# Eight heads instead of four on the partitions for Q and the output of a linear attention, with more stores held back

## The chip, the cores and the metric

The kernel runs on one core of a Trainium2 chip. The metric is the device time of one execution in microseconds (us), which is lower when better. Times are medians of several runs. A profile shows one execution, and its span is 1.8 us shorter than that execution's time (129.1 of 130.87 us before). The engines are PE (matrix multiply), DVE (VectorE), ACT (ScalarE), POOL (GpSimd) and SP (SyncE). In the profile of the kernel before, GpSimd's transfers stand in a queue of the kind software (q0, 20.98 MB) and SP's and ACT's in two of the kind hardware (q1, 10.49 MB, and q10, 0.52 MB). Their packets took 81.7%, 21.7% and 1.1% of the time of the same 16 DMA engines; that is over 100% together, since packets overlap.

## The reference

```python
# Q, K, V: (8, 12, 512, 64) float32
Q_feat = np.maximum(0, Q)
K_feat = np.maximum(0, K)
KV = np.einsum('bhkd,bhkv->bhdv', K_feat, V)
K_sum = np.sum(K_feat, axis=2)
numerator = np.einsum('bhqd,bhdv->bhqv', Q_feat, KV)
denominator = np.einsum('bhqd,bhd->bhq', Q_feat, K_sum)
out = numerator / (denominator[:, :, :, None] + 1e-10)
```

There are 96 heads. The work per byte is small: 37.7 MB are read and 12.6 MB written.

## The kernel before

Four heads make a group, and there are 24 groups. A group's Q, K, V and output lie on 128 partitions, 32 partitions a head, so each partition holds one contiguous row of 4 KB in HBM. The loads cast to bf16 and are issued by GpSimd. PE computes K-transposed times V for the group (line 120, 32 matmuls), transposes Q (line 135, 8), and multiplies (line 150, 32). A column of ones beside V gives the denominator.

```python
def load_kv(g):                                   # ... K, V: [P, 16 rows, 64] bf16
    nc.gpsimd.dma_start(out=k_sb[g].rearrange("p r d -> p (r d)"), in_=Kr[g])
    ...
def mm_kv(g):
    for r in range(R):                            # R = 16
        for t in range(2):                        # two halves of 64 partitions
            ts_ = slice(64 * t, 64 * t + 64)
            nc.tensor.matmul(ps_kv[g][:, t, 0:D1],
                kf[g][ts_, r, :, :].rearrange("p s d -> p (s d)"),
                vo[g % NB][ts_, r, :],
                start=(r == 0), stop=(r == R - 1), skip_group_check=True)
def mm_out(g):
    for j in range(2):
        ...
            for h in range(NHG):                  # 4 heads, one strip of 32 columns each
                hs = slice(32 * h, 32 * h + 32)
                nc.tensor.matmul(po[hs, v // 2, ...], qt[g][:, u, hs],
                    kvd[g % NB][:, h // 2, h % 2, :, :],
                    start=True, stop=True, skip_group_check=True)
def store(g, o_sb):
    if NG - 2 - HELD <= g < NG - 2:               # HELD = 5
        nc.gpsimd.dma_start(out=Or[g], ...)       # behind all loads, in GpSimd's program
    elif g == NG - 1:
        ...                                       # two halves, nc.sync
    else:
        nc.sync.dma_start(out=Or[g], ...)
```

Stores of five late groups are "held": GpSimd issues them after the last load, so that they do not compete with loads that the computation needs: in the trace a group takes 3.75 us where loads run alone and 5.11 us where stores run beside them.

## Time and profile before

| | before |
|---|---|
| time, median (3 runs) | 131.06 us |
| span in the profile | 129.1 us |
| PE busy, instructions (matmuls; as many weight loads) | 76.5 us, 1728 |
| granted PE clock (mean share of full speed) | 0.573 |
| HBM read, written | 37.75 MB, 12.58 MB |

The first lines of the page of the kernel before: busy time by engine, then the granted clock and the DMA engines' busy share in 40 slices (9 is 90% or more), and further down the chain that ended last.

```profile
PE 76.5 (59%) x1728; PEld 57.0 (44%) x1728; DVE 79.8 (62%) x230; ACT 51.1 (40%) x121; POOL 45.1 (35%) x81
...
PEclk9999955555555555555555555555555555555785
DMA  4999999999999999999999999999999999999972
...
DMA 86%; issue 3%; PE 3%; POOL 2%; DVE 2%; ACT 2%; ACTq 0%; POOLq 0%
```

No compute engine is over 62% busy, the DMA engines are full from the second slice to the 38th, and the chain is DMA. The kernel is bound by its transfers.

Windows of the kernel before (start and end, length, busy time of each engine with its count of instructions, then granted clock, DMA share, GB/s as counted at the landing side, where a load counts as bf16, half of what it reads from HBM: the packets of the whole run hold 32.23 MB, where 50.3 MB were read and written in HBM; a share above 1, such as 1.12 from 108 to 110 us, says that the times of packets overlap).

```profile
120.00:122.00 2.00, 1.67 (x40) 1.29 (x32) 1.35 (x6) 1.05 (x5) 0.24 (x1) 0.67 1.00 399
122.00:124.00 2.00, 0.64 (x32) 0.46 (x32) 1.31 (x4) 0.79 (x1) 0.00 (x0) 1.00 0.70 285
124.00:126.00 2.00, 0.00 (x0) 0.00 (x0) 1.40 (x4) 0.00 (x0) 0.00 (x0) 0.68 0.82 329
126.00:128.00 2.00, 0.00 (x0) 0.00 (x0) 0.00 (x0) 0.00 (x0) 0.00 (x0) 0.50 0.41 157
```

In the last 6 us the DMA engines have a hole: the last groups' stores come one by one as they are computed.

### The profile page before, as it was taken

The numbers are of one execution on the slowest core, as the hardware profiler recorded it, in microseconds if no ns is written. First come the engines' busy times: TensorE is split into PE (matmuls) and PEld (weight loads), VectorE is DVE, ScalarE is ACT, GpSimd is POOL, SyncE is SP. The second block draws the span as 40 slices with busy tenths as digits, with TensorE's granted clock in tenths as the row PEclk, the third lists the DMA queues.
The fourth block names the chain that finished last, engine by engine and source line by source line (L and its number), as shares of the span: only waits on it lengthen the run. The fifth ranks groups of instructions, "written<-read, shape, count | busy, mean of one in ns | idle before, by whom it ended". The sixth has DMA issues, their size and how long they took to land.

```text
span 129.1 us, 4091 instructions
## 1 busy us (share of the span) xinstructions
PE 76.5 (59%) x1728; PEld 57.0 (44%) x1728; DVE 79.8 (62%) x230; ACT 51.1 (40%) x121; POOL 45.1 (35%) x81
## 2 busy tenths in 40 slices
PE   0068476547576585485675755855756458887610
PEld 0057354425444363364454544633644336665410
DVE  1283775737757558467476584584673849889660
ACT  3027535433345334433543453344335253652700
POOL 6945343133333315224333243152331335311100
PEclk9999955555555555555555555555555555555785
DMA  4999999999999999999999999999999999999972
GB/s 118 305 209 209 211 171 274 277 219 285 229 269 272 226 285 250 245 286 239 258 282 225 275 262 234 285 249 248 285 230 267 273 227 206 212 216 368 388 307 111
DMA packets 13986, 32.23 MB, mean 250 GB/s; under 512 B 1553, under 2 KB 1553, under 8 KB 13969
## 3 DMA queue, kind: packets, MB, share of 16 engines
q0 software_dynamic: 10800, 20.98, 81.7%
q1 hardware_dynamic: 3024, 10.49, 21.7%
q10 hardware_dynamic: 144, 0.52, 1.1%
q8 instruction: 13, 0.21, 0.6%
q14 instruction: 5, 0.03, 0.1%
HBM read 37.75 MB, written 12.58 MB: 390 GB/s over the span
## 4 chain that ended last, share of the span: by engine, by line
DMA 86%; issue 3%; PE 3%; POOL 2%; DVE 2%; ACT 2%; ACTq 0%; POOLq 0%
DMA q_sb<-in_Q_dram 38%; DMA k_sb<-in_K_dram 27%; DMA v_sb<-in_V_dram 21%; ACT qt L139 2%; PE ps_qt L135 1%; PE ps_out L150 1%; DVE o_sb L164 1%; POOL q_sb L80 0%; POOL v_sb L76 0%; POOL k_sb L74 0%; DVE rec L163 0%; POOL ident masks.py:199 0%; DVE den L161 0%; POOL ident masks.py:197 0%; ACTq L139 0%
## 5 line engine op out<-in xcount | busy, mean ns | idle before, releaser
L120 PE MATMUL ps_kv<-vo,kf 64*128 64x65 bf16 x768 | 25.1, 239 | 36.3 <-DVE vo L112 34.4
L120 PEld LDWEIGHTS <-kf 64*128 64x128 bf16 x768 | 21.4, 126 | 42.0 <-DVE vo L112 34.3
L129 ACT CAST kvd<-ps_kv 64x130 bf16<-64x130 f32 x96 | 25.3, 264 | 36.1 <-PE ps_kv L120 34.2
L139 ACT ACTIVATE qt<-ps_qt 128x1024 bf16<-128x1024 bf16 x24 | 24.6, 1023 | 33.8 <-PE ps_qt L135 33.8
L110 DVE TENSOR_SCALAR kf<-k_sb,mask 128x1024 bf16<-128x1024 bf16 x46 | 20.3, 483 | 27.2 <-DMA k_sb<-in_K_dram 27.2
L150 PE MATMUL ps_out<-kvd,qt 128*32 128x130 bf16 x768 | 28.8, 303 | 10.0 <-DVE o_sb L164 6.9
L164 DVE TENSOR_TENSOR o_sb<-ps_out,rec 128x512 f32<-128x512 f32 x48 | 33.2, 692 | 1.7
L80 POOL DMA_DIRECT2D q_sb<-in_Q_dram x24 | 17.2, 715 | 36.0 <-DMA k_sb<-in_K_dram 34.7
L150 PEld LDWEIGHTS <-qt 128*32 128x32 bf16 x768 | 17.4, 127 | 18.8 <-DVE o_sb L164 12.5
L135 PE MATMUL ps_qt<-ident,q_sb 128*128 128x128 bf16 x192 | 24.3, 306 | 0.7 <-DMA q_sb<-in_Q_dram 0.7
L135 PEld LDWEIGHTS <-q_sb 128*128 128x128 bf16 x192 | 18.1, 139 | 5.5 <-issue 4.4
L76 POOL DMA_DIRECT2D v_sb<-in_V_dram x23 | 12.3, 533 | 19.3 <-DMA q_sb<-in_Q_dram 15.0
L74 POOL DMA_DIRECT2D k_sb<-in_K_dram x23 | 12.4, 541 | 11.8 <-DMA v_sb<-in_V_dram 8.9
L112 DVE COPY vo<-v_sb 128x1024 bf16<-128x1024 bf16 x23 | 9.9, 431 | 8.5 <-DMA v_sb<-in_V_dram 8.5
L163 DVE RECIPROCAL rec<-den 128x8 f32<-128x8 f32 x48 | 9.7, 203 | 1.7
L161 DVE TENSOR_SCALAR den<-ps_out 128x8 f32<-128x8 f32 x48 | 7.5, 157 | 1.7 <-PE ps_out L150 1.7
L174 POOL DMA_DIRECT2D out_dram<-o_sb x5 | 2.7, 549 | 7.8 <-DVE o_sb L164 6.2
L110 DVE TENSOR_SCALAR kf<-k_first,mask 128x1024 bf16<-128x1024 f32 x2 | 1.4, 751 | 3.8 <-DMA k_first<-in_K_dram 3.8
L129 ACT ACT_TABLE_LOAD x1 | 1.3, 1283 | 1.8 <-DVE kvd L103 1.8
L101 DVE MEMSET mask<- 32x1 f32 x8 | 0.3, 59 | 0.9 <-PEq L213 0.8
L103 DVE MEMSET kvd<- 128x260 f32 x3 | 0.8, 275 | 0.0
L112 DVE CAST vo<-v_first 128x1024 bf16<-128x1024 f32 x1 | 0.7, 692 | 0.0
(7 smaller groups left out, 1.1 us busy)
## 6 DMA issues: line engine op xcount, KB each, us to landing
out_dram<-o_sb SPq DMA_DIRECT2D x18, 512.0 KB, 6.9
q_sb<-in_Q_dram POOLq DMA_DIRECT2D x24, 256.0 KB, 12.4
k_sb<-in_K_dram POOLq DMA_DIRECT2D x23, 256.0 KB, 13.7
v_sb<-in_V_dram POOLq DMA_DIRECT2D x23, 256.0 KB, 13.7
out_dram<-o_sb POOLq DMA_DIRECT2D x5, 512.0 KB, 9.6
v_first<-in_V_dram ACTq DMA_DIRECT2D x1, 512.0 KB, 4.8
k_first<-in_K_dram SPq DMA_DIRECT2D x1, 512.0 KB, 4.7
out_dram<-o_sb SPq DMA_DIRECT2D x2, 256.0 KB, 2.4
```

Source lines behind the costliest of these rows:

```text
L74: nc.gpsimd.dma_start(out=k_sb[g].rearrange("p r d -> p (r d)"), in_=Kr[g])
L76: nc.gpsimd.dma_start(out=v_sb[g].rearrange("p r d -> p (r d)"), in_=Vr[g])
L80: nc.gpsimd.dma_start(out=q_sb[g].rearrange("p u f -> p (u f)"), in_=Qr[g])
L110: nc.vector.tensor_scalar(kf[g][:, :, s, :], k_sb[g], scalar1=0.0, scalar2=mask[:, s:s + 1], op0=Alu.max, op1=Alu.mult)
L112: nc.vector.tensor_copy(vo[g % NB][:, :, 0:D], v_sb[g])
L120: nc.tensor.matmul(ps_kv[g][:, t, 0:D1], kf[g][ts_, r, :, :].rearrange("p s d -> p (s d)"), vo[g % NB][ts_, r, :], start=(r == 0), stop=(r ...
L129: nc.scalar.copy(kvd[g % NB][64 * c:64 * c + 64, :, s, c, :], ps_kv[g][64 * s:64 * s + 64, :, 0:D1])
L135: nc.tensor.transpose(ps_qt[g][:, u, :], q_sb[g][:, u, :], ident)
L139: nc.scalar.activation(qt[g].rearrange("p u q -> p (u q)"), ps_qt[g].rearrange("p u q -> p (u q)"), Act.Relu)
L150: nc.tensor.matmul(po[hs, v // 2, (v % 2) * 2 * D1:(v % 2) * 2 * D1 + 2 * D1], qt[g][:, u, hs], kvd[g % NB][:, h // 2, h % 2, :, :], start ...
L163: nc.vector.reciprocal(rec, den)
L164: nc.vector.tensor_tensor(o_sb[:, 8 * j:8 * j + 8].rearrange("p (b r) d -> p b r d", b=2), pv[:, :, :, 0:D], rec.unsqueeze(3).to_broadcast ...
```

## The change

The intent: longer rows for half of the bytes (Q and output in "octets" of eight heads, 16 partitions a head, 8 KB rows), and more stores held behind the loads to fill the hole at the end. A strip of 32 PE columns now holds two heads. So the transposed Q is written twice, each time with the other head's columns zero, and two matmuls accumulate: 1536 output matmuls instead of 768. The diff, cut to its core:

```diff
-    NHG = 4
-    R = S * NHG // P
-    U = R // 2
+    R = S * 4 // P                      # K, V: 16
+    RQ = S * 8 // P                     # Q, out: 32
+    U = RQ // 2
+    NO = NG // 2                        # 12 octets
+    F32 = 2
-    qin = pool("qin", NG)
-    kin = pool("kin", 20)
-    outp = pool("outp", 10)
+    qin = pool("qin", 7)
+    kin = pool("kin", 12)
+    outp = pool("outp", HELD + 2)       # 8 KB tiles, HELD = 5 octets
...
+    for g in range(F32):                # K, V of groups 0 and 1 in fp32, by SP and ACT
+        nc.sync.dma_start(out=k_sb[g]..., in_=Kr[g])
+        nc.scalar.dma_start(out=v_sb[g]..., in_=Vr[g])
...
+    def evac_qt(o, i):
+        for z in range(2):              # the other head's columns stay zero
+            nc.scalar.activation(qtz[o % NZ][:, z, us, :, z, :], pv[:, :, :, z, :], Act.Relu)
...
-                for h in range(NHG):
+            for z in range(2):
+                for w in range(4):
+                    h = 2 * w + z
                     nc.tensor.matmul(
                         po[hs, v // 2, ...],
-                        qt[g][:, u, hs],
-                        kvd[g % NB][:, h // 2, h % 2, :, :],
-                        start=True, stop=True, skip_group_check=True)
+                        qtf[o % NZ][:, z, u * P + 32 * w:u * P + 32 * w + 32],
+                        kvd[(2 * o + h // 4) % NK][:, h % 4 // 2, h % 2, :, :],
+                        start=(z == 0), stop=(z == 1), skip_group_check=True)
...
-        if NG - 2 - HELD <= g < NG - 2:
+        if NO - 1 - HELD <= o < NO - 1:
```

More of the change, by code (lines that the diff above doesn't have):

```diff
@@ L24 @@
     NH = B * H
+    R = S * 4 // P
+    RQ = S * 8 // P
     NHG = 4
-    R = S * NHG // P
-    U = R // 2
+    U = RQ // 2
     NG = NH // NHG
-    assert NG * NHG == NH and R == 16
+    NO = NG // 2
+    assert NO * 8 == NH and R == 16 and RQ == 32
     HELD = 5
+    F32 = 2
     fp32 = mybir.dt.float32
@@ L41 @@
     consts = pool("consts", 1)
-    qin = pool("qin", NG)
-    kin = pool("kin", 20)
-    vin = pool("vin", 20)
+    qin = pool("qin", 7)
+    kin = pool("kin", 12)
+    vin = pool("vin", 12)
     kfp = pool("kfp", 3)
-    qtp = pool("qtp", 3)
     rcp = pool("rcp", 4)
-    outp = pool("outp", 10)
+    outp = pool("outp", HELD + 2)
     pkv = pool("pkv", 1, space=bass.MemoryType.PSUM)
@@ L51, with view @@
     pou = pool("pou", 2, space=bass.MemoryType.PSUM)
-    def rview(X):
-        return X.rearrange("b h s d -> (b h s d)").rearrange("(n p f) -> n p f", p=P, f=R * D)
-    Qr, Kr, Vr, Or = rview(Q), rview(K), rview(V), rview(out)
+    def view(X, f):
+        return X.rearrange("b h s d -> (b h s d)").rearrange("(n p f) -> n p f", p=P, f=f)
+    Qr, Kr, Vr, Or = view(Q, RQ * D), view(K, R * D), view(V, R * D), view(out, RQ * D)
     ident = consts.tile([P, P], bf16, name="ident")
     NB = 3
+    NK = 4
+    NZ = 2
     vo = [consts.tile([P, R, D1], bf16, name=f"vo{i}") for i in range(NB)]
-    kvf = [consts.tile([P, NHG * 2 * D1], bf16, name=f"kvd{i}") for i in range(NB)]
+    kvf = [consts.tile([P, NHG * 2 * D1], bf16, name=f"kvd{i}") for i in range(NK)]
     kvd = [x.rearrange("p (t s c d) -> p t s c d", t=2, s=2, c=2) for x in kvf]
     mask = consts.tile([P, 2], fp32, name="mask")
+    qtf = [consts.tile([P, 2, U * P], bf16, name=f"qt{i}") for i in range(NZ)]
+    qtz = [x.rearrange("p z (u w y c) -> p z u w y c", u=U, w=4, y=2) for x in qtf]
     ctx.enter_context(tc.manual_schedule())
@@ L76, in load_kv, with load_q @@
         nc.gpsimd.dma_start(out=v_sb[g].rearrange("p r d -> p (r d)"), in_=Vr[g])
-    def load_q(g):
-        q_sb[g] = qin.tile([P, U, 2 * D], bf16, name="q_sb")
-        nc.gpsimd.dma_start(out=q_sb[g].rearrange("p u f -> p (u f)"), in_=Qr[g])
-    k_sb[0] = outp.tile([P, R, D], fp32, name="k_first", tag="o_sb")
-    nc.sync.dma_start(out=k_sb[0].rearrange("p r d -> p (r d)"), in_=Kr[0])
-    v_sb[0] = outp.tile([P, R, D], fp32, name="v_first", tag="o_sb")
-    nc.scalar.dma_start(out=v_sb[0].rearrange("p r d -> p (r d)"), in_=Vr[0])
+    def load_q(o):
+        q_sb[o] = qin.tile([P, U, 2 * D], bf16, name="q_sb")
+        nc.gpsimd.dma_start(out=q_sb[o].rearrange("p u f -> p (u f)"), in_=Qr[o])
+    for g in range(F32):
+        kv = outp.tile([P, 2, R, D], fp32, name="kv_first", tag="o_sb")
+        k_sb[g], v_sb[g] = kv[:, 0], kv[:, 1]
+        nc.sync.dma_start(out=k_sb[g].rearrange("p r d -> p (r d)"), in_=Kr[g])
+        nc.scalar.dma_start(out=v_sb[g].rearrange("p r d -> p (r d)"), in_=Vr[g])
     load_q(0)
     make_identity(nc, ident)
-    for g in range(1, NG - 2):
-        load_kv(g)
-        load_q(g)
-    load_kv(NG - 2)
-    load_kv(NG - 1)
-    load_q(NG - 2)
-    load_q(NG - 1)
+    for o in range(1, NO):
+        load_kv(2 * o)
+        load_kv(2 * o + 1)
+        load_q(o)
     def zero(i):
@@ L101, in zero, with zero_q @@
                     nc.vector.memset(mask[32 * h:32 * h + 32, s:s + 1], 1.0 if h % 2 == s else 0.0)
-        nc.vector.memset(vo[i][:, :, D:D1], 1.0)
+        if i < NB:
+            nc.vector.memset(vo[i][:, :, D:D1], 1.0)
         nc.vector.memset(kvf[i].bitcast(fp32), 0.0)
-    kf, qt, ps_kv, ps_qt, ps_out = {}, {}, {}, {}, {}
+    def zero_q(i):
+        nc.vector.memset(qtf[i].rearrange("p z f -> p (z f)").bitcast(fp32), 0.0)
+    kf, ps_kv, ps_qt, ps_out = {}, {}, {}, {}
     def prep(g):
@@ L128, in evac_kv @@
             for c in range(2):
-                nc.scalar.copy(kvd[g % NB][64 * c:64 * c + 64, :, s, c, :],
+                nc.scalar.copy(kvd[g % NK][64 * c:64 * c + 64, :, s, c, :],
                                ps_kv[g][64 * s:64 * s + 64, :, 0:D1])
-    def transp(g):
-        ps_qt[g] = pqt.tile([P, U, P], bf16, name="ps_qt")
-        for u in range(U):
-            nc.tensor.transpose(ps_qt[g][:, u, :], q_sb[g][:, u, :], ident)
-    def evac_qt(g):
-        qt[g] = qtp.tile([P, U, P], bf16, name="qt")
-        nc.scalar.activation(
-            qt[g].rearrange("p u q -> p (u q)"), ps_qt[g].rearrange("p u q -> p (u q)"), Act.Relu)
@@ L142, in mm_out, with transp @@
-    def mm_out(g):
-        for j in range(2):
-            po = pou.tile([P, 2, 512], fp32, name="ps_out")
-            ps_out[g, j] = po
-            for v in range(U // 2):
-                u = j * (U // 2) + v
-                for h in range(NHG):
-                    hs = slice(32 * h, 32 * h + 32)
+    def transp(o, i):
+        ps_qt[o, i] = pqt.tile([P, U // 2, P], bf16, name="ps_qt")
+        for u in range(U // 2):
+            nc.tensor.transpose(ps_qt[o, i][:, u, :], q_sb[o][:, i * (U // 2) + u, :], ident)
@@ new lines, in evac_qt, with mm_out @@
+    def evac_qt(o, i):
+        us = slice(i * (U // 2), (i + 1) * (U // 2))
+        pv = ps_qt[o, i].rearrange("p u (w y c) -> p u w y c", w=4, y=2)
+        for z in range(2):
+            nc.scalar.activation(qtz[o % NZ][:, z, us, :, z, :], pv[:, :, :, z, :], Act.Relu)
+    def mm_out(o, j):
+        po = pou.tile([P, 2, 512], fp32, name="ps_out")
+        ps_out[o, j] = po
+        for v in range(4):
+            u = 4 * j + v
+            for z in range(2):
+                for w in range(4):
+                    hs = slice(32 * w, 32 * w + 32)
+                    h = 2 * w + z
@@ L150, in mm_out @@
                     nc.tensor.matmul(
                         po[hs, v // 2, (v % 2) * 2 * D1:(v % 2) * 2 * D1 + 2 * D1],
-                        qt[g][:, u, hs],
-                        kvd[g % NB][:, h // 2, h % 2, :, :],
-                        start=True, stop=True, skip_group_check=True)
-    def norm(g):
-        o_sb = outp.tile([P, R, D], fp32, name="o_sb", tag="o_sb")
-        for j in range(2):
-            pv = ps_out[g, j][:, :, 0:4 * D1].rearrange("p b (r d) -> p b r d", d=D1)
-            den = rcp.tile([P, 2, 4], fp32, name="den")
-            nc.vector.tensor_scalar(den, pv[:, :, :, D], scalar1=1e-10, scalar2=None, op0=Alu.add)
-            rec = rcp.tile([P, 2, 4], fp32, name="rec")
-            nc.vector.reciprocal(rec, den)
-            nc.vector.tensor_tensor(
-                o_sb[:, 8 * j:8 * j + 8].rearrange("p (b r) d -> p b r d", b=2),
-                pv[:, :, :, 0:D],
-                rec.unsqueeze(3).to_broadcast([P, 2, 4, D]), op=Alu.mult)
-        return o_sb
@@ L172, in store, with norm @@
-    def store(g, o_sb):
-        if NG - 2 - HELD <= g < NG - 2:
-            nc.gpsimd.dma_start(out=Or[g], in_=o_sb.rearrange("p r d -> p (r d)"))
-        elif g == NG - 1:
+                        qtf[o % NZ][:, z, u * P + 32 * w:u * P + 32 * w + 32],
+                        kvd[(2 * o + h // 4) % NK][:, h % 4 // 2, h % 2, :, :],
+                        start=(z == 0), stop=(z == 1), skip_group_check=True)
+    def norm(o, j, o_sb):
+        pv = ps_out[o, j][:, :, 0:4 * D1].rearrange("p b (r d) -> p b r d", d=D1)
+        den = rcp.tile([P, 2, 4], fp32, name="den")
+        nc.vector.tensor_scalar(den, pv[:, :, :, D], scalar1=1e-10, scalar2=None, op0=Alu.add)
+        rec = rcp.tile([P, 2, 4], fp32, name="rec")
+        nc.vector.reciprocal(rec, den)
+        nc.vector.tensor_tensor(
+            o_sb[:, 8 * j:8 * j + 8].rearrange("p (b r) d -> p b r d", b=2),
+            pv[:, :, :, 0:D],
+            rec.unsqueeze(3).to_broadcast([P, 2, 4, D]), op=Alu.mult)
@@ L176, in store @@
+    def store(o, o_sb):
+        if NO - 1 - HELD <= o < NO - 1:
+            nc.gpsimd.dma_start(out=Or[o], in_=o_sb.rearrange("p r d -> p (r d)"))
+        elif o == NO - 1:
             for j in range(2):
-                rs = slice(R // 2 * j, R // 2 * (j + 1))
-                nc.sync.dma_start(out=Or[g].rearrange("p (r d) -> p r d", d=D)[:, rs],
+                rs = slice(RQ // 2 * j, RQ // 2 * (j + 1))
+                nc.sync.dma_start(out=Or[o].rearrange("p (r d) -> p r d", d=D)[:, rs],
@@ L179, in store @@
                                   in_=o_sb[:, rs])
         else:
-            nc.sync.dma_start(out=Or[g], in_=o_sb.rearrange("p r d -> p (r d)"))
+            nc.sync.dma_start(out=Or[o], in_=o_sb.rearrange("p r d -> p (r d)"))
     zero(0)
     prep(0)
-    for g in range(NG):
-        mm_kv(g)
-        evac_kv(g)
-        if g + 1 < NG:
-            if g + 1 < NB:
-                zero(g + 1)
-            prep(g + 1)
-        if g > 0:
-            mm_out(g - 1)
-            store(g - 1, norm(g - 1))
-        transp(g)
-        evac_qt(g)
@@ L197 @@
-    mm_out(NG - 1)
-    store(NG - 1, norm(NG - 1))
+    zero(1)
+    zero_q(0)
+    o_sb = {}
+    for o in range(NO + 1):
+        for i in range(2):
+            g = 2 * o + i
+            if o < NO:
+                mm_kv(g)
+                evac_kv(g)
+                if g + 1 < NG:
+                    prep(g + 1)
+                if g == 0:
+                    for k in range(2, NK):
+                        zero(k)
+                    zero_q(1)
+            if o > 0:
+                if i == 0:
+                    o_sb[o - 1] = outp.tile([P, RQ, D], fp32, name="o_sb", tag="o_sb")
+                for j in (2 * i, 2 * i + 1):
+                    mm_out(o - 1, j)
+                    norm(o - 1, j, o_sb[o - 1])
+        if o > 0:
+            store(o - 1, o_sb[o - 1])
+        if o < NO:
+            for i in range(2):
+                transp(o, i)
+                evac_qt(o, i)
```

## The prediction

> **What bounds the kernel now.** The DMA engines. The chain of waits is 86% DMA (Q 38%, K 27%, V 21%), and in the 40-slice table DMA is at 9 tenths from the second slice to the 38th. No compute engine is over 62% busy. The HBM side moves 50.3 MB (37.75 read, 12.58 written). In the timeline, loads alone (108 to 116 us, stores held) take 3.75 us for a group's 1.57 MB, 419 GB/s; with stores a group (2.10 MB) takes 5.11 us, 410 GB/s, which leaves about 402 GB/s for the mixed share (estimate). The windows show three losses: about 2.2 us before the engines are full; 122 to 127 us, where DMA share falls to 0.67-0.90 because each last store waits for its computation (estimate 2.2 us lost with the gaps around it); and 2 us from the last bytes at 127 us to the end.
>
> **What the change does.**
> 1. Held stores grow from 2.6 to 5.2 MB. After the last load the kernel has that plus the last octet, some 15 us of transfers, to cover the last octet's computation (estimate 7 to 8 us: transposes, eviction, four output stages paced by 1.05 us of normalisation each). The tail hole nearly closes: -2.0 us. Less mixing of reads and writes: -0.3 us.
> 2. Q and out rows grow from 4 KB to 8 KB, so half the bytes have half as many descriptors. At 419 GB/s a 4 KB row costs an engine 156 ns[...]. This trace has no 8 KB row to confirm it.[...]
> 3. K and V of group 1 in fp32 by the other queues: nothing starts earlier; preparing them takes 2.1 us against 1.3, and two clearings of 128x2048 an estimated 2.2 us each (scaled from 275 ns for 260). All under the load stream: 0 at the end.
> 4. Output matmuls double to 1536 (zero padding). At the granted clock of 0.5, 32 take 1.06 us. An octet then needs PE 2.1 + 4.2 + 2.1 = 8.4 us, DVE 6.8, ACT some 4.7. An octet of mixed traffic takes 10.2 us, of loads alone 7.5. So compute falls about 1 us per octet behind in the held half, 5 us at most, hidden by the 15 us of stores. Not on the critical path.
>
> **Sum.** 131.06 - 2.0 - 0.3[...] - 0.3 (small) = 127.6 us. Range 125.2 to 130.3. Chances: faster 0.66, same 0.31, slower 0.03.
>
> **What would show it.** Right: DMA full to within about 2.5 us of the end; loads end near 108 us and stores alone follow for some 14 us; load-only rate 420 GB/s or a little over; the chain ends in DMA rather than in PE, ACT and DVE pieces; half as many packets for Q and out. Wrong, step 1: DMA share under 0.9 for over 2 us in the last 10. Step 2: no higher rate in like stretches. Step 4: PE busy over 90% with loads waiting on buffers.
>
> **What could upset it.** An octet of compute above 9.5 us[...] would make compute end last, 2 to 5 us later;[...] stores alone may run slower than the 400 GB/s seen.

One term of the sum goes, that of step 2 (longer rows); with it the sum came to 127.6 us. The first two terms are estimates from the trace: 2.0 us out of the 2.2 that the first paragraph counts as lost near the end, and 2.6 MB at 402 GB/s against 419 GB/s, which differ by 0.26 us. The last 0.3 (small) is the author's estimate without a source. In step 4 the octet's 8.4, 6.8 and 4.7 us are estimates as well: at the clock of 0.5 the trace has 1.06 us for 32 K-V matmuls and 1.03 us for 8 transposes, and DVE and ACT were busy 6.7 and 4.3 us for two groups (79.8 and 51.1 us for 24).

## More of the kernel before

The two longest waits of PE in the kernel before: which instruction group waited, for whom, total us, times, longest.

```profile
PE ps_kv L120 <- DVE vo L112: 34.4, 19, 7.6
PE ps_out L150 <- DVE o_sb L164: 6.9, 21, 0.5
```

PE waits for V to be prepared, that is, for data to arrive: the preparation by DVE itself waited 27.2 us for loads of K and 8.5 us for loads of V. No wait of PE is put down to "issue", time in which an engine waited for nothing that the profile shows.

## The result and the profile after

The changed kernel took 135.69 us (median of 4 runs, 135.04 to 135.92) against 130.93 us for the kernel before: slower by 3.5%, ratio 1.0353, 95% interval 1.0311 to 1.0395. A ratio here is the mean time of one kernel's fast runs over that of the other's fast runs of the same rounds, so it is not quite the ratio of the medians. Executions over 1.5% slower than the fastest of the same kernel are left out of the means.

The same lines of the page, changed kernel (span 133.8 us):

```profile
PE 76.9 (58%) x2496; PEld 64.8 (48%) x2496; DVE 83.4 (62%) x233; ACT 50.5 (38%) x145; POOL 34.8 (26%) x67
...
PEclk9999998685569959599555599599995599686896
DMA  4999999999999999999999999999999999870563
...
PE 48%; issue 29%; DVE 11%; DMA 7%; ACT 2%; SPq 0%; ACTq 0%
```

PE's busy time barely rose: its granted clock was 0.80 in this execution against 0.57, and the 192 transposes, which did not change, took 20.3 us against 24.3. But the chain is no longer DMA (7%). It is PE (48%) and "issue" (29%), time in which PE waited for nothing that the profile names. The waits of PE say the same; there was no such line before:

```profile
PE ps_out L165 <- issue: 25.0, 12, 3.4
PE ps_kv L131 <- DVE vo L123: 12.0, 3, 7.5
PE ps_kv L131 <- issue: 8.2, 4, 2.9
PE ps_qt L147 <- issue: 3.3, 1, 3.3
```

That is 36.5 us of unexplained pauses in PE. And the end now has a real hole: windows of the changed kernel.

```profile
119.00:121.00 2.00, 0.85 (x41) 0.65 (x44) 0.53 (x3) 0.00 (x0) 0.00 (x0) 1.00 0.33 139
121.00:123.00 2.00, 2.00 (x69) 1.62 (x70) 1.71 (x6) 1.06 (x4) 0.00 (x0) 0.58 0.05 16
123.00:125.00 2.00, 1.85 (x30) 1.46 (x32) 0.85 (x2) 1.29 (x3) 0.53 (x1) 0.56 0.02 4
125.00:127.00 2.00, 1.14 (x76) 0.99 (x72) 1.37 (x6) 0.77 (x2) 0.00 (x0) 1.00 0.96 385
```

From 121 to 125 us the DMA engines had nothing to do: loads were done, all held stores that were computed were out, and the last two octets were still being computed.

Where do the pauses stand? The timeline of PE in the changed kernel (start, length, instruction group, count, and in brackets the idle time ahead):

```profile
42.76 0.59 PE L131 MATMUL ps_kv<-vo,kf 64*128 64x65 bf16 x26
46.23 0.35 PE L131 MATMUL ps_kv<-vo,kf 64*128 64x65 bf16 x6 [2.88 <-issue]
46.51 1.93 PE L165 MATMUL ps_out<-kvd,qt 128*32 128x130 bf16 x64
48.36 1.06 PE L131 MATMUL ps_kv<-vo,kf 64*128 64x65 bf16 x32
49.35 0.69 PE L165 MATMUL ps_out<-kvd,qt 128*32 128x130 bf16 x25
52.50 0.71 PE L165 MATMUL ps_out<-kvd,qt 128*32 128x130 bf16 x36 [2.45 <-issue]
```

The pauses fall in the middle of groups: 26 of 32 matmuls run, PE stops for almost 3 us, and the other 6 follow. The program has no wait there. From one pause to the next this view counts 6 + 64 + 32 + 25 = 127 matmuls, each with its weight load. With two semaphore instructions of PE's own, which the trace also records there, that makes 256 PE instructions.

So I counted PE's instruction records in the trace (matmuls, weight loads, semaphore instructions). The first such pause comes after 449 records, and each of the next 16 begins exactly 256 records after the last. The DMA records fit: the page lists a queue of kind "instruction". Before, then after:

```profile
q8 instruction: 13, 0.21, 0.6%
```

```profile
q8 instruction: 19, 0.31, 0.8%
```

Each packet is 16384 bytes. I read a packet of q8 as a block of 256 PE instructions. No record says so, but the times fit: PE's records have 18 such borders and the queue 19 packets, and in each of the 17 pauses PE goes on 2.2 to 2.5 us after a packet's start. The 17 pauses on block borders are 40.5 us together from the start of the record before each to the start of the one after, of which PE is idle for 36.5. In the changed kernel these packets start every 6.14 us (median), and each takes 0.9 to 1.0 us. The packet itself starts some 3.7 us (median) after PE has entered the block before, here 1.7 us at the least and in the kernel before 0.8 us at the least. In none of the traces does it start earlier than that entry. So a block comes some 6.1 us after PE has entered the one before, and by then that one has long run out: PE was through it in 3.9 us (median). In the kernel before, the packets also start 3.6 us (median) after PE enters a block, but there PE takes 9.2 us for 256 instructions, and nothing waits.

**Theory F (fetch).** With the data queues full, PE gets no more than one block of 256 instructions per 6.15 us. An octet of the changed kernel has 416 PE instructions, so it takes 416/256 x 6.15 = 10.0 us. The transposes of successive octets are in fact 10.00 us apart (mean over the octets from the second on). A group before had 144 PE instructions: 3.5 us, less than the 5.1 us of its transfers.

**Theory W (work).** The doubled matmul work and its coupling to DVE and ACT makes an octet 10 us long; the border pauses are where it shows.

**Theory R (rows).** 8 KB rows slow the transfers or the queues.

### The profile page after: what moved, and what is told of

It is laid out like the page before. It is cut to its first block, busy times and chain, and to the rows that moved or that the text cites. A ratio compares the mean times of both kernels' runs of the same rounds, so it can differ in the third digit from the quotient of the medians.

```text
span 133.8 us, 5622 instructions
## 1 busy us (share of the span) xinstructions
PE 76.9 (58%) x2496; PEld 64.8 (48%) x2496; DVE 83.4 (62%) x233; ACT 50.5 (38%) x145; POOL 34.8 (26%) x67
## 4 chain that ended last, share of the span: by engine, by line
PE 48%; issue 29%; DVE 11%; DMA 7%; ACT 2%; SPq 0%; ACTq 0%
PE ps_out L165 22%; PE ps_qt L147 13%; PE ps_kv L131 13%; DMA kv_first<-in_K_dram 7%; DVE o_sb L177 5%; DVE kf L121 2%; DVE rec L176 1%; ACT kvd L140 1%; DVE qt L114 1%; DVE den L174 1%; ACT qt L153 1%; DVE vo L123 1%; DVE kvd L111 0%; SPq L95 0%; DVE vo L110 0%
## 5 line engine op out<-in xcount | busy, mean ns | idle before, releaser
L165 PE MATMUL ps_out<-kvd,qt 128*32 128x130 bf16 x1536 | 38.1, 255 | 27.6 <-issue 25.0
L165 PEld LDWEIGHTS <-qt 128*32 128x32 bf16 x1536 | 29.2, 113 | 31.4 <-issue 25.1
L153 ACT ACTIVATE qt<-ps_qt 128x512 bf16<-128x512 bf16 x48 | 24.9, 602 | 36.1 <-PE ps_qt L147 36.1
L131 PE MATMUL ps_kv<-vo,kf 64*128 64x65 bf16 x768 | 22.0, 217 | 20.5 <-DVE vo L123 12.0
L131 PEld LDWEIGHTS <-kf 64*128 64x128 bf16 x768 | 18.3, 111 | 26.8 <-issue 13.2
L147 PE MATMUL ps_qt<-ident,q_sb 128*128 128x128 bf16 x192 | 20.3, 289 | 3.3 <-issue 3.3
L89 POOL DMA_DIRECT2D q_sb<-in_Q_dram x12 | 6.7, 557 | 18.2 <-DMA v_sb<-in_V_dram 16.7
L121 DVE TENSOR_SCALAR kf<-kv_first,mask 128x1024 bf16<-128x1024 f32 x4 | 2.8, 752 | 3.9 <-DMA kv_first<-in_K_dram 3.8
L114 DVE MEMSET qt<- 128x2048 f32 x2 | 3.5, 1765 | 0.8 <-issue 0.8
L123 DVE CAST vo<-kv_first 128x1024 bf16<-128x1024 f32 x2 | 1.4, 706 | 0.0
```

Of the source, the lines that this page charges most:

```text
L121: nc.vector.tensor_scalar(kf[g][:, :, s, :], k_sb[g], scalar1=0.0, scalar2=mask[:, s:s + 1], op0=Alu.max, op1=Alu.mult)
L123: nc.vector.tensor_copy(vo[g % NB][:, :, 0:D], v_sb[g])
L131: nc.tensor.matmul(ps_kv[g][:, t, 0:D1], kf[g][ts_, r, :, :].rearrange("p s d -> p (s d)"), vo[g % NB][ts_, r, :], start=(r == 0), stop=(r ...
L147: nc.tensor.transpose(ps_qt[o, i][:, u, :], q_sb[o][:, i * (U // 2) + u, :], ident)
L153: nc.scalar.activation(qtz[o % NZ][:, z, us, :, z, :], pv[:, :, :, z, :], Act.Relu)
L165: nc.tensor.matmul(po[hs, v // 2, (v % 2) * 2 * D1:(v % 2) * 2 * D1 + 2 * D1], qtf[o % NZ][:, z, u * P + 32 * w:u * P + 32 * w + 32], kvd[ ...
```

## The experiments

All runs named below were made beside runs of the kernel before on the same chip, 130.8 to 130.9 us in each job (median). The changed kernel was timed in a job of its own, so a difference from it is one between jobs. This table of my own counting from the traces gathers what theory F is about: instruction packets, their median distance, the pauses of PE on borders of 256 instructions (over 0.6 us from the start of one record to the start of the next, so some 0.2 us of each is work), and the mean distance of a transposition of Q from the next (an octet; for kernels with groups, a group).

```
kernel      packets  distance us  border pauses, sum us   period us
before         13        8.9            0,  0.0           4.95 a group
after          19        6.14          17, 40.5          10.00 an octet
half           13        7.5            1,  1.1           9.17 an octet
narrow         19        6.05          17, 40.8           9.92 an octet
rows4k         19        6.12          16, 34.3           9.98 an octet
b_extra        19        6.22          13, 21.9           5.16 a group
b_extra16      16        6.56           1,  0.7           4.93 a group
fewloads       19        3.97          11, 15.1           6.94 an octet
a_wide0        16        6.10          11, 18.5           8.66 an octet
```

### half: the second matmul of each pair left out

```diff
-            for z in range(2):
+            for z in range(1):                 # wrong result on purpose; start and stop both True
```

> The changed kernel with only the first of each pair of zero-padded output matmuls (wrong result on purpose: half of the heads come out as zero). PE instructions fall from 4992 to 3456. Theory F (PE's instruction blocks of 256 are delivered no faster than one per 6.15 us while the data queues are full): an octet has 288 PE instructions, 6.9 us of delivery, less than its 7.5 us of loads; the pauses of 2 to 3.5 us in the middle of matmul groups nearly vanish, the kernel is bound by DMA again and takes 126.5 to 129 us, which is also what the blind prediction would give without its miss. Theory W (the doubled matmul work itself, 128 matmuls per octet, delays the chain): faster too, so this run does not part F from W, but sizes both. Theory R (8 KB rows make the transfers or the queues slower): no change, about 135.7 us.

Measured: 130.11 us, ratio to before 0.9943 (0.9928 to 0.9958). The doubling of the output matmuls costs 5.6 us of the 135.7 (a difference of medians from two jobs, each with before at 130.9). With it gone, the pauses are gone but for one, and PE waits for V again:

```profile
PE ps_kv L131 <- DVE vo L123: 31.2, 18, 7.6
```

The overlap at the end shows it too. In the changed kernel the last load landed at 110.7 us and PE finished at 128.4, 17.7 us later; in half these are 110.3 and 117.3, 7.0 us. But 130.1 is above my 126.5 to 129: something besides the doubling was wrong in the prediction.

### narrow: the same count, half the columns

```diff
+                    nw = 2 * D1 if z == 0 else 2      # wrong result on purpose
-                        kvd[...][:, h % 4 // 2, h % 2, :, :],
+                        kvd[...].rearrange("p c d -> p (c d)")[:, 0:nw],
```

> The changed kernel with all 1536 output matmuls, but the second of each pair streams 2 columns and not 130 (wrong result on purpose). As many PE instructions, about half the column work in that group. Theory F: pauses stay, one per 256 PE instructions, blocks still 6.1 to 6.2 us apart, time 135 to 136.4 us, while PE busy falls by over 8 us. Theory W: an octet is 2 us shorter, time 3 us or more below the changed kernel's, 132.5 or less. Theory R: no change, but it has no reason for PE busy to fall without effect.

Measured: 135.23 us, ratio 1.0334 (1.0309 to 1.0358), within 0.5 us of the changed kernel. PE's timeline in narrow:

```profile
46.65 0.35 PE L131 MATMUL ps_kv<-vo,kf 64*128 64x65 bf16 x6 [1.39 <-issue]
46.93 1.25 PE L166 MATMUL ps_out<-kvd,qt 128*32 128x130 bf16 x64
...
52.85 0.35 PE L166 MATMUL ps_out<-kvd,qt 128*32 128x130 bf16 x14 [2.90 <-issue]
```

A run of 64 output matmuls now takes 1.25 us against 1.93 in the changed kernel's timeline above. The saving went into the pauses: the next block comes at 52.85 us, where it came at 52.50. Theory W predicted 132.5 or less and is out. One thing that I expected did not show: PE busy fell by 1.9 us, not by over 8. The mean granted clock was lower here (0.66 against 0.80), and what had not changed took longer: the 768 K-V matmuls 24.9 us against 22.0.

### rows4k: the changed kernel with 4 KB transfers

```diff
-        nc.gpsimd.dma_start(out=q_sb[o]..., in_=Qr[o])
+        for j in range(2):                     # half a row each; stores likewise
+            nc.gpsimd.dma_start(out=qf[:, cs], in_=Qr[o][:, cs])
```

> The changed kernel with each Q load and each store issued as two transfers of 4 KB rows; compute untouched. Theory F: about 135.7 us, within 1 us, because delivery of PE's instruction blocks still bounds; if the block interval depends on the size of the rows queued ahead of it, it drops from 6.15 us and the time with it. Theory W: within 1 us of 135.7. Theory R: clearly faster, 133 us or less. It also shows what 8 KB rows were worth: the load-only rate from 12 to 20 us against the 210 to 212 GB/s (as landed in bf16) of the changed kernel; I expect less than 1% difference.

Measured: 136.84 us (136.50 over the three fast runs), ratio 1.0467 (1.0435 to 1.0498); one of the four runs was slow, and the three fast ones spread from 135.17 to 137.17. It is not faster, so theory R is out, and the distance of the blocks is the same (6.12 us), so it does not hang on the size of the rows. The trace prices the rows: a Q packet takes 324 ns as 8 KB and 173 ns as 4 KB, so two short rows take 346. That is 6% for those bytes, some of it hidden by overlap: from 12 to 20 us, with loads alone, the rate is 212 GB/s with long rows and 210 with short ones, at DMA shares of 1.11 and 1.12. The long rows help a little, as predicted; they cannot be what slowed the kernel.

### b_extra and b_extra16: instructions added to the kernel before

```diff
+                    for nw in (2, 2 * D1):     # b_extra16: only for h < 2
                         nc.tensor.matmul(
-                            po[hs, ...:... + 2 * D1], qt[g][:, u, hs], kvd[...],
+                            po[hs, ...:... + nw], qt[g][:, u, hs], kvd[...][:, 0:nw],
                             start=True, stop=True, skip_group_check=True)
```

> The kernel before, with a matmul of 2 columns put ahead of each of its 768 output matmuls (overwritten by the full one, result correct). PE instructions 3456 to 4992, nothing else changed: rows of 4 KB, no zero padding, one octet layout less. Theory F: a group then has 208 PE instructions, 5.0 us of delivery: little change while loads and stores mix (5.1 us a group), but the stretch with held stores cannot go at 3.75 us a group any more; pauses at 256-instruction borders appear; time 133 to 137 us. Theory W: the extra column work is small (2 columns against 130), so within 1.5 us of 131. Theory R: 131, no change.

> Half the dose of b_extra: a 2-column matmul ahead of every second output matmul, 176 PE instructions a group, 4.2 us of delivery at 6.15 us per 256. Theory F: well below the 5.1 us of a mixed group, above the 3.75 us of a group of loads alone, so only the held stretch and the end suffer: 131.5 to 133 us, less than half of the 4.3 us that the full dose cost. A cost per added matmul, wherever it stands, would give half of it: 133.1.

Measured: b_extra 135.21 us, ratio 1.0331 (1.0311 to 1.0350), result correct; b_extra16 131.05 us, ratio 1.0034 (1.0005 to 1.0064). Adding 768 matmuls of 2 columns to the old layout reproduces the loss, with nothing else of the change in it. The waits of PE in b_extra now have the lines that the kernel before had not:

```profile
PE ps_kv L120 <- DVE vo L112: 23.4, 18, 7.6
PE ps_out L151 <- issue: 10.2, 9, 2.0
PE ps_kv L120 <- issue: 5.3, 3, 3.1
PE ps_qt L135 <- issue: 3.6, 2, 2.3
```

Half the dose costs 0.3 us by the medians, not half of 4.3. In b_extra16 256 instructions took PE 6.7 us (median), longer than the 6.14 us between blocks in the changed kernel and the 6.22 us in b_extra, and one border pause was left (0.7 us) where b_extra has 13 (21.9 us). A price for each added matmul or weight load, wherever it stands, does not fit this. (I had expected 131.5 to 133 for it, so delivery has more slack in the held stretch than I reckoned.)

### fewloads: are the blocks late because the data queues are full?

```diff
-    for o in range(1, NO):
+    for o in range(1, 3):                      # wrong result on purpose
         load_kv(2 * o); load_kv(2 * o + 1); load_q(o)
+    for o in range(3, NO):                     # later octets read tiles of octets 1 and 2
+        ...
```

> The changed kernel with loads for the first three octets only; later octets read the tiles of octets 1 and 2 again (wrong result on purpose). Loads fall from 37.7 to about 9.4 MB, so from some 30 us on the data queues are mostly empty, while PE has the same 4992 instructions in the same order. If the 6.15 us per block of PE instructions is waiting behind queued data: the interval falls to what PE takes to run 256 instructions (some 4 to 5.5 us), the pauses at block borders fall under 1 us, and the time falls to 90 to 115 us. If it is a fixed cost of fetching: intervals stay at 6.1 us or more, pauses stay, and the time stays above 128 us.

Measured: 105.03 us in a single run, whose state is unknown. The median distance of the blocks fell from 6.14 to 3.97 us (least 3.46), with the same instructions in the same order. So a good part of the 6.15 us comes from the traffic. Not all: 11 pauses remained, with a mean of 1.4 us, where I had expected under 1. At a granted clock of 1.0 PE runs 256 such instructions in an estimated 2.2 us (64 output matmuls with their weight loads took 1.12 us early in the changed kernel), less than the 3.46 us between blocks that was the least here, with little traffic. The packets' starts tell which part the traffic adds: from PE's entering a block to the start of the next block's packet it is 1.6 us here (median) against 3.7, while from there to PE's going on it is 2.3 us in both. So between these two runs the traffic lengthened the wait before the packet starts, and not what follows. Why the rest takes 2.3 us, of which the packet is 0.9 to 1.0, these traces do not show.

### b_held10 and b_held7, b_gate10 and b_gate7: the tail by itself

```diff
-    HELD = 5
+    HELD = 10                                  # or 7; kin, vin 12 (16), outp 15 (12)
```

```diff
+            if g == NG - 2 - HELD:             # b_gate: the held stores go to SP's queue,
+                nc.sync.dma_start(out=gate, in_=k_sb[NG - 1][:, 0, 0:8])
-            nc.gpsimd.dma_start(out=Or[g], ...)
+            nc.sync.dma_start(out=Or[g], ...)
```

> The kernel before with ten groups of stores held (5.2 MB, as many bytes as in the changed kernel) and not five; 12 buffers for K and V instead of 20, 15 for outputs instead of 10. This is step 1 of the prediction alone, with 144 PE instructions a group (3.5 us of delivery against 3.75 us of loads). By the prediction 128.7 to 129.2 us. If the last engine's lag at the end (4.4 us between the first and the last of the 16 engines in the run called half) eats most of it: 129.8 to 130.8.

> The kernel before with seven groups of stores held, 16 buffers for K and V, 12 for outputs. By the prediction about 1 us off the 130.9 of before; if the lag between engines eats the gain, 130.0 to 131.

> As b_held10 (ten groups of stores held, rows of 4 KB), but the held stores are issued by SyncE behind a copy of 16 bytes a partition that waits for the K of the last group, so that GpSimd's own queue ends with the loads. In b_held10 the last byte landed at 127.3 us and GpSimd reported ready only at 130.7, 3.3 us later, and every engine waited for that. If that end of GpSimd is what made b_held10 2.4 us slower than before: 130.0 to 131.3 us, GpSimd no longer last. If holding more costs in some other way: 132.5 to 133.5 us.

> The same with seven groups held. If GpSimd's end is the cost: 129.5 to 131 us against the 132.0 of b_held7; otherwise about 132.

| run | median | ratio to before (95%) |
|---|---|---|
| b_held7 | 132.01 us | 1.0090 (1.0076 to 1.0105) |
| b_held10 | 133.25 us | 1.0188 (1.0174 to 1.0202) |
| b_gate7 | 130.73 us | 0.9996 (0.9982 to 1.0011) |
| b_gate10 | 130.54 us | 0.9977 (0.9961 to 0.9993) |

Both expectations for b_held were wrong: holding more made the old kernel slower. The waits of SP's own queue at the end of the program show why, first in b_held10, then in b_gate10.

```profile
SPq L224 <- DMA out_dram<-o_sb: 8.1, 2, 6.8
SPq L224 <- PEq L224: 3.4, 2, 2.9
```

```profile
SPq L227 <- DMA out_dram<-o_sb: 3.7, 4, 1.4
SPq L227 <- PEq L227: 0.7, 2, 0.5
```

After all stores had landed, SP waited another 2.9 us in the barrier that ends the program; with the held stores on SP's queue it waited 0.5. The view names PE as the releaser, but in the records PE was long done and GpSimd came last. In b_held10 the last store that GpSimd had issued landed at 127.3 us, and GpSimd reached the barrier at 130.7. In the run half the same wait was up to 1.4 us. Since moving those stores to SP's queue took the loss back (133.25 to 130.54), although the last byte landed later there (127.9 us), the end of GpSimd's own queue is its cause; what GpSimd does in those 3.3 us is not in the trace.

b_gate10 is then the test of step 1 of the prediction without that end, and its answer is 0.3 us. The hole did fill. Windows of b_gate10:

```profile
120.00:122.00 2.00, 0.00 (x0) 0.00 (x0) 0.00 (x0) 0.00 (x0) 0.00 (x0) 0.50 1.02 408
122.00:124.00 2.00, 0.00 (x0) 0.00 (x0) 0.00 (x0) 0.00 (x0) 0.00 (x0) 0.50 1.03 412
124.00:126.00 2.00, 0.00 (x0) 0.00 (x0) 0.00 (x0) 0.00 (x0) 0.00 (x0) 0.50 1.00 390
126.00:129.00 3.00, 0.00 (x0) 0.00 (x0) 0.00 (x0) 0.00 (x0) 0.00 (x0) 0.50 0.09 35
```

But from 120 to 126 us this kernel moved 2.42 MB and still had 0.1 MB left, while before moved only 2.03 MB in the same time and had 0.3 MB left: b_gate10 came to 120 us with more to do. The packets, counted on the HBM side, show where it lost this. From 109 to 111 us, where the loads end and SP's stores begin behind the gate, they fall from 418 GB/s to 295 and 314 (an estimated 0.5 us lost); with stores alone, from 112 to 124 us, they run at 397 to 412 GB/s, where b_held10's run at 408 to 421. (The 369 GB/s that the window from 110 to 115 us gives at the landing side still has loads in it, until 111.7 us.) So the gate has a price of its own, and b_gate10 is not step 1 alone. But b_held10 has no gate, and there too the last byte landed only 0.35 us earlier than before (127.31 us against 127.66). With more stores queued the 16 engines ended further apart: 3.95 us between the first and the last on the last store of GpSimd in b_held10, 1.5 us on the last store in b_gate10, 0.35 us before. The hole was exchanged for a ragged end.

### a_wide0 and a_wide_gate: fewer PE instructions, correct

```diff
 def mm_kv(g):
         for r in range(R):
-            for t in range(2):
-                ts_ = slice(64 * t, 64 * t + 64)
-                nc.tensor.matmul(ps_kv[g][:, t, 0:D1], kf[g][ts_, r, ...], vo[g % NB][ts_, r, :], ...)
+            nc.tensor.matmul(ps_kv[g]..., kf[g][:, r, ...], vo[g % NB][:, r, :, :]..., ...)
 # V of partitions 0..63 goes to columns 0..64, of partitions 64..127 to 65..129, the rest is zero
+        for t in range(2):
+            ts_ = slice(64 * t, 64 * t + 64)
+            nc.vector.tensor_copy(vo[g % NB][ts_, :, t, 0:D], v_sb[g][ts_])
```

The cut leaves out that the three V tiles are cleared at the start and that the K-V products lie in a smaller PSUM tile.

> The changed kernel, result correct, with the K-V product done in 16 matmuls of 128 partitions by 130 columns a group in place of 32 of 64 by 65 (V written block-wise into a zeroed tile). PE instructions 4992 to 4224, 352 an octet: 8.5 us of delivery against 10.0. PE column work rises, not falls[...], and DVE gets one more copy of 0.43 us a group. Theory F: faster than the changed kernel in spite of more work, 131 to 133.5 us, with 16 blocks fetched in place of 19. Theory W: slower than the changed kernel, 137 us or more.

> a_wide0, and the held stores of octets issued by SyncE behind a small copy that waits for the last group's K (so GpSimd ends with the loads), and the clearings moved ahead of the first K and V. An attempt at a version that beats both kernels: 8 KB rows, fewer PE instructions than the changed kernel, no late end of GpSimd. If the three causes found so far (instruction delivery, GpSimd's end, nothing else) are all: 128.5 to 130.3 us, against 130.8 of before. If above 131, something is still missing.

Measured: a_wide0 128.47 us, ratio to before 0.9817 (0.9795 to 0.9840: clear of noise, but unclear whether it is 2%); a_wide_gate 129.03 us, ratio 0.9858 (0.9836 to 0.9880). Both are correct. a_wide0 is the changed kernel with 768 PE instructions fewer, and it is 7.2 us faster, although PE is busy longer in the group concerned and as long in all (76.5 us against 76.9), as the page of each shows (busy us and mean ns behind the bar). The changed kernel, then a_wide0:

```profile
L131 PE MATMUL ps_kv<-vo,kf 64*128 64x65 bf16 x768 | 22.0, 217 | 20.5 <-DVE vo L123 12.0
```

```profile
PE 76.5 (60%) x2112; PEld 64.8 (51%) x2112; DVE 97.0 (77%) x263; ACT 50.7 (40%) x145; POOL 35.9 (28%) x67
...
PEclk9999999999999599968999999955999999999855
DMA  3999999999999999999999999999999999999983
...
DVE 45%; PE 20%; DMA 18%; issue 12%; ACT 1%; DVEq 0%; ACTq 0%
...
L134 PE MATMUL ps_kv<-vo,kf 128*128 128x130 bf16 x384 | 31.9, 246 | 23.8 <-DVE vo L128 23.0
```

An octet takes 8.66 us; delivery of its 352 instructions at 6.15 us a block would be 8.46. Work, 6.4 us of PE busy time an octet (76.5 us over 12), did not bind; the mean clock was 0.92. (That clock and the smaller PSUM tile were not tried apart from the count.) The granted clock did not follow PE's busy share: PE was busy for 59%, 58% and 60% of the span with mean clocks of 0.57 before, 0.80 changed and 0.92 here, and other executions of the kernel before had clocks from 0.57 to 0.96, all at 130.5 to 131.2 us. So the clock did not set the time of the kernel before, and what sets the clock stays open. DVE grew to 97.0 us and now has the largest part of the chain, 45%.

a_wide_gate, which I had expected to be the best, is 0.6 us worse. It differs in two ways (held stores on SP's queue, clearings before the first preparation, whose first product came at 9.6 us instead of 8.3). They were not tried apart, and a_wide0's GpSimd did not come last (SP waited 0.5 us at most in its final barrier, as in b_gate10), so the gate had nothing to gain. a_wide0 is the fastest version: 1.8% below the kernel before, 5.3% below the changed one (128.47 against 135.69).

## Why the prediction was wrong

- **What bounds the kernel before**: right. The changed kernel is no longer bound by it, which the prediction excluded.
- **Step 4, "Output matmuls double to 1536 ... Not on the critical path"**: this step failed. It costed the 768 added matmuls by their time in PE, 1.06 us for 32, and that was about right: 64 took 1.93 us. It left out that they are also 1536 more instructions to fetch. Delivery at one block per 6.15 us makes an octet 10.0 us where I reckoned 8.4, hence a chain of PE with 36.5 us of pauses. The overlap that I counted on failed with it: compute was to fall 5 us behind the loads at most, hidden by 15 us of stores; PE finished 17.7 us after the last load, against 7.0 us in half, which is 10.7 us behind. half shows the size, 5.6 us; narrow shows that the work of the matmuls is not it; b_extra makes the same loss in the old layout; a_wide0 takes it away with fewer instructions and as much busy time. "What could upset it" did name an octet above 9.5 us, with compute ending last and 2 to 5 us lost, but not because of the number of instructions. The sign that it gave for step 4 (PE busy over 90%) was wrong too: PE was busy 58%.
- **Step 1, "The tail hole nearly closes: -2.0 us", with -0.3 for less mixing**: mis-sized. In the changed kernel it could not happen, since compute ended last. In the kernel before it measured -0.3 us in total with the held stores on SP's queue (b_gate10, the gate's price included) and +2.4 us with them on GpSimd's (b_held10). What it overlooked is that in b_held10 the DMA engines ended 3.95 us apart, against 0.35 us before, and that GpSimd was ready only 3.3 us after its last store had landed.
- **Step 2, 8 KB rows**: right in sign: loads alone ran at 212 GB/s against 210 (rows4k) or 211 (before), and a Q packet took 324 ns against 346 for the same bytes in two, 22 ns less; the overlap of packets (DMA share 1.11) hides part of that. No correct kernel bound by DMA isolates it.
- **Step 3, the start**: it was to be 0 at the end, under the load stream. In half, which DMA bounds, no piece of it is on the chain. In the changed kernel PE's chain runs from the start, and one clearing (1.5 of its 1.76 us, where 2.2 were predicted) lies on it.
- **Sum**: 135.7 measured less 127.6 predicted is 8.1 us. 5.6 are step 4. The other 2.5 are what half lacks to the prediction (130.1 against 127.6), about the -2.3 that step 1 did not bring; the rest of that account, GpSimd's end in half (up to 1.4 us) against the rows' gain, is an argument and was not measured apart.

## What to carry to other kernels

Count the instructions of PE as well as its time: where the transfers keep the queues full, compare some 6.15 us per 256 instructions (6.14 in the changed kernel, 6.22 in b_extra) with the time in which PE would otherwise run them, and look for idle time put down to "issue" in the middle of matmul groups, at equal counts. Where the count is too high, try fewer and larger matmuls even if they stream zeros; here that won 7.2 us (a_wide0). Do not end a program with large stores on GpSimd's queue without looking at who comes last to the final barrier: ten groups of held stores took 133.25 us there and 130.54 us on SP's queue.
